# Two weight buffers of their own for the modulation vectors, fetched two ahead, and five instead of six for the rest

## Chip, cores and metric

The kernel runs on 1 core of one Trainium2 chip. The metric is the device time of one execution in microseconds (us), taken as the median of several runs.

## What is computed

The reference runs two blocks over a residual stream x of 256 tokens by 1024 features, with a second stream (the context) beside it, all in float32. Its parts are gated feed-forward networks (FFN), a short convolution mixer, a sparse attention that shares its keys and values ("kv"), a differential attention and a grouped-query attention. Each sublayer is modulated by vectors that come from a conditioning vector c:

```python
def modulate_pre(x, g_pre, shift, scale):
    return rms_norm(x, g_pre) * (1.0 + scale[:, None, :]) + shift[:, None, :]

def gated_post_add(x, y, g_post, gate, weight):
    return x + weight * gate[:, None, :] * rms_norm(y, g_post)

def swiglu_ffn(h, w_in, w_out):
    g, u = jnp.split(h @ w_in, 2, axis=-1)
    return (jax.nn.silu(g) * u) @ w_out

    shift, scale = jnp.split(jax.nn.silu(c) @ kv_ada_w + kv_ada_b, 2, axis=-1)
```

Shift, scale and gate are all products silu(c) @ W + b with W of 1024 by 1024 for each vector. The change concerns how these W (inputs `ada_w` and `kv_ada_w`) are brought in.

## The kernel before

**The large products** run on PE. A float32 weight block of 128 x 1024 (512 KB) is brought in by one DMA into a raw buffer (`raw_half`, line 237, issued from SP), split into a rounded high part by ACT (`whi`, line 246) and a remainder by DVE (`wlo`, line 247), and each product takes three matmuls: high by high, high by low and low by high (lines 492 to 494, 510 to 514). `slab` makes two such blocks and then calls `tick`. The raw pool has 6 buffers.

**The modulation vectors** are made on DVE. `gemv` puts eight steps for each vector in a queue, one for each block of 128 x 1024 of W; there are 32 vectors, 256 steps. A step is one scalar_tensor_tensor of DVE (line 176) for each condition: weight times `srow` (silu(c) on all partitions), summed along the row into one column of `vec`. 48 of the steps have two conditions, so line 176 issues 304 such instructions. The full product goes into a scratch tile `vjunk` (bf16, one buffer) that nobody reads. Sixteen more such instructions stand in `first_ffn` (line 311). After the eighth step a bias is added (line 180). `tick` adds credit at a rate that depends on the stage (`CFG`), and takes a step when there is enough; `need` forces the steps that are still missing when a vector is used. `step` uses the weight that the step before it had fetched, and fetches the next one (line 169 to 171), so one weight is on its way ahead. These fetches use the same raw pool and the same SP queue as the weights of the products.

**The order on each engine** is fixed when the program is built, by a scheduler that goes by priorities and free buffers; `slab` puts its loads and splits 36 places earlier (`early`). An engine carries out its instructions in that order, each waiting for its own inputs and buffers. SP issues nearly all weight DMAs, and its waits for a free raw buffer are in this queue as well. The context stream is woven into the main one by the program's writing (tiles with "ctx" in their name).

**Names in rows:** a00, a01, a02 are the first layer's FFN, convolution and FFN, kv the shared keys and values, a10, a11, a12 the second layer, diff0 the differential attention, bffn0 and bffn2 the FFNs of the second block, gqa its last attention. A tile's name has its stage and a running number. Lines touched: `step`, `fetch`, `tick` (152 to 182), pools (89 to 97), `first_ffn` (310), `grow` (369), `kv_cmp` (746), `late_setup` (1175).

## Time and profile before

| | |
|---|---|
| Median of 3 runs | 2145.55 us (2139.5 to 2145.56) |
| Profiled execution | 2140.95 us, of which the profiled span is 2139.2 us |
| Mean granted TensorE clock | 0.979 |
| PE busy | 2013.3 us, 94% of the span |
| DVE busy | 1625.5 us, 76% |
| ACT busy | 1087.3 us, 51% |
| DMA queue of the weights | 477.90 MB, 63.7% of 16 DMA engines |

The profile gives, for each engine, busy time and the idle time before an instruction with the work that ended it. A share of the span is an average over stages; the rows further below are from single places.

### The profile page before, as it was taken

The numbers are of one execution on the slowest core, as the hardware profiler recorded it, in microseconds if no ns is written. First come the engines' busy times: TensorE is split into PE (matmuls) and PEld (weight loads), VectorE is DVE, ScalarE is ACT, GpSimd is POOL, SyncE is SP. The second block draws the span as 40 slices with busy tenths as digits, with TensorE's granted clock in tenths as the row PEclk, the third lists the DMA queues.
The fourth block names the chain that finished last, engine by engine and source line by source line (L and its number), as shares of the span: only waits on it lengthen the run. The fifth ranks groups of instructions, "written<-read, shape, count | busy, mean of one in ns | idle before, by whom it ended". The sixth has DMA issues, their size and how long they took to land. (4 is left out here: it accounts for less than half of the span.)

```text
span 2139.2 us, 34672 instructions
## 1 busy us (share of the span) xinstructions
PE 2013.3 (94%) x13158; PEld 1796.2 (84%) x13158; DVE 1625.5 (76%) x2753; ACT 1087.3 (51%) x1769; POOL 133.6 (6%) x188
## 2 busy tenths in 40 slices
PE   6999899999899899899999999999999998989998
PEld 5998797998789788787788989877789997768998
DVE  7878898777877688878978666789888656866554
ACT  4444545443444466656765444547754444555443
POOL 0000201000200000110000000210010001100000
PEclk9999999999999999989999999999999999999999
DMA  8989697988677766544566866554359755414553
GB/s 332 330 309 355 236 327 277 330 292 291 222 258 276 241 230 210 195 157 138 190 238 232 292 221 237 180 207 148 128 207 342 264 191 178 140 53 150 188 186 118
DMA packets 136327, 486.46 MB, mean 227 GB/s; under 512 B 14976, under 2 KB 16480, under 8 KB 135392
## 3 DMA queue, kind: packets, MB, share of 16 engines
q1 hardware_dynamic: 134240, 477.90, 63.7%
q0 software_dynamic: 1728, 6.29, 0.8%
q8 instruction: 103, 1.69, 0.3%
q14 instruction: 64, 0.52, 0.1%
q10 hardware_dynamic: 192, 0.05, 0.0%
HBM read 480.47 MB, written 3.19 MB: 226 GB/s over the span
## 5 line engine op out<-in xcount | busy, mean ns | idle before, releaser
L1049 ACT ACT_TABLE_LOAD x15 | 19.2, 1283 | 6.6 <-DVE dst.diff0.2984_16079 L1047 1.7
L340 ACT ACT_TABLE_LOAD x13 | 16.7, 1283 | 0.2
L273 PE MATMUL ps.a00.6_101<-ident,x 128*128 128x128 f32 x4 | 1.1, 427 | 13.8 <-DMA x<-in_x 13.8
L375 POOL DMA_DIRECT2D G.bffn0.3378_18457<-row.bffn0.3377_18455 x1 | 0.6, 595 | 198.4 <-DMA row.bffn0.3377_18455<-diag.bffn0.3376_18453 198.4
L273 PEld LDWEIGHTS ps.a00.6_101<-ident,x 128*128 128x128 f32 x4 | 0.7, 216 | 13.7 <-issue 13.7
L375 POOL DMA_DIRECT2D G.a02.1032_5643<-row.a02.1031_5641 x1 | 0.6, 595 | 182.2 <-DMA row.a02.1031_5641<-diag.a02.1030_5639 182.2
L734 ACT ACTIVATE chunk.kv.1231_6595<-chunk.kv.1128_6071,cols 128x60 f32<-128x60 f32 x32 | 9.8, 387 | 4.0 <-PE ps.a10.1253_6672 L744 4.0
L375 POOL DMA_DIRECT2D G.a12.2528_13717<-row.a12.2527_13715 x1 | 0.6, 595 | 180.2 <-DMA row.a12.2527_13715<-diag.a12.2526_13713 180.2
L333 ACT ACT_TABLE_LOAD x9 | 11.5, 1283 | 0.2
L375 POOL DMA_DIRECT2D G.bffn2.3890_21467<-row.bffn2.3889_21465 x1 | 0.6, 595 | 171.6 <-DMA row.bffn2.3889_21465<-diag.bffn2.3888_21463 171.6
L401 POOL TENSOR_TENSOR rv.ctx.354_2048<-ss.ctx.352_2044,epsd 128x1 f32<-128x1 f32 x1 | 0.2, 191 | 169.8 <-ACT junk.ctx.351_2043 L394 169.8
L375 POOL DMA_DIRECT2D G.a11.2165_11615<-row.a11.2164_11613 x1 | 0.5, 530 | 116.9 <-DMA row.a11.2164_11613<-diag.a11.2163_11611 116.9
L484 ACT CAST chunk.a01.490_2583<-chunk.a01.492_2585 128x256 fp32r<-128x256 f32 x8 | 3.2, 406 | 8.9 <-DVE chunk.a01.492_2585 L676 8.9
L287 PE MATMUL ps.a00.38_198<-chunk.a00.20_148,chunk.a00.34_188 128*128 128x256 f32 x8 | 3.2, 401 | 4.8 <-ACT chunk.a00.34_188 L299 2.9
L386 POOL TENSOR_TENSOR rr.ctx.1396_7610<-rv.ctx.1395_7608,nhalf 128x8 f32<-128x8 f32 x1 | 1.6, 1637 | 87.7 <-DVE rv.ctx.1395_7608 L382 87.7
L176 DVE SCALAR_TENSOR_TENSOR vjunk.a12.2456_13210<-raw.a12.2435_13097,srow 128x1024 bf16<-128x1024 f32 x1 | 1.2, 1226 | 7.4 <-DMA raw.a12.2435_13097<-in_ada_w 7.4
L287 PEld LDWEIGHTS ps.a00.38_198<-chunk.a00.20_148,chunk.a00.34_188 128*128 128x128 f32 x8 | 2.0, 254 | 5.7 <-ACT chunk.a00.34_188 L299 3.2
L982 PE MATMUL ps.ctx.1412_7672<-ident,chunk.ctx.453_2431 128*128 128x128 f32 x4 | 1.1, 428 | 5.9 <-DVE chunk.ctx.453_2431 L962 5.9
L869 ACT ACT_TABLE_LOAD x5 | 6.4, 1283 | 0.1
L492 PE MATMUL ps.a10.1241_6626<-chunk.kv.1219_6556,whi.a10.1244_6630 128*128 128x256 f32 x8 | 3.1, 392 | 3.1 <-ACT whi.a10.1244_6630 L246 3.1
L982 PEld LDWEIGHTS ps.ctx.1412_7672<-ident,chunk.ctx.453_2431 128*128 128x128 f32 x4 | 0.7, 218 | 6.3 <-issue 6.3
L386 POOL TENSOR_TENSOR rqc<-rv.ctx.1316_7145,nhalf 128x8 f32<-128x8 f32 x1 | 1.6, 1637 | 62.0 <-DVE rv.ctx.1316_7145 L382 62.0
(11975 smaller groups left out, 9434.4 us busy)
## 6 DMA issues: line engine op xcount, KB each, us to landing
srow<-in_crow SPq DMA_DIRECT2D x3, 512.0 KB, 4.6
x<-in_x SPq DMA_DIRECT2D x1, 1024.0 KB
xc<-in_ctx SPq DMA_DIRECT2D x1, 1024.0 KB
kvd<-chunk.ctx.452_2429 SPq DMA_DIRECT2D x1, 1024.0 KB, 8.3
kvd<-chunk.ctx.451_2428 SPq DMA_DIRECT2D x1, 1024.0 KB
chunk.diff0.2745_14861<-kvd SPq DMA_DIRECT2D x1, 1024.0 KB
chunk.diff0.2746_14862<-kvd SPq DMA_DIRECT2D x1, 1024.0 KB
out<-x SPq DMA_DIRECT2D x2, 512.0 KB, 2.6
```

Of the source, the lines that this page charges most:

```text
L273: nc.tensor.transpose(ps[:, k, t * P:(t + 1) * P], self.x[:, t, kt * P:(kt + 1) * P], self.ident)
L287: mm(out, whi[:, ks], hi[:, k], start=(k == 0), stop=False)
L333: nc.scalar.activation(sg, gate, AF.Silu)
L340: nc.scalar.activation(sg, gate, AF.Silu)
L375: nc.gpsimd.dma_start(G, src.to_broadcast([P, D]))
L386: nc.gpsimd.tensor_tensor(r, v, self.nhalf[:, 0:n], op=ALU.pow)
L484: nc.scalar.copy(hi, src)
L492: mm(out, shi, mhi, start=first, stop=False)
L734: nc.scalar.activation(bt[:, j], self.kv2[i][:, :, 2 * j:2 * j + 16 * (NCMP - 1) + 1:16], AF.Identity, bias=self.col("pos", 16 * i + j, 1))
L869: nc.scalar.activation(p[:, br], p[:, br], AF.Exp, bias=mx[:, par, br:br + 1], accum_out=sm[:, br, par:par + 1])
L982: nc.tensor.transpose(ps[:, j, :], src[:, j * P:(j + 1) * P], self.ident)
L1049: nc.scalar.activation(e[:, :nk], ps[:, :nk], AF.Exp, bias=st[:, m:m + 1], scale=r, accum_out=st[:, 2 + m:3 + m])
```

## The change

The weights of the modulation vectors get a pool `vraw` with two buffers. `fetch` now fills a list of up to two weights and is called at the start and at the end of `step`, so two weights are on their way; the DMAs stay on SP (line 167 of the changed kernel). The load of weight n+2 waits until the last scalar_tensor_tensor on weight n is done. The raw pool of the other weights goes from 6 to 5 buffers. The scratch product is written over the weight itself, in float32, or, for the first of two conditions, into a tile `G` (two buffers, shared with the gate rows of `grow`). To make room, `vjunk` is gone, `diag` goes from two buffers to one, and the tile `misc` is replaced by a slot of `sg`, the tile that the FFN's gating uses. Numbers of instructions stay the same on every engine.

```diff
--- before.py
+++ after.py
@@ -87,7 +87,8 @@
         self.tc, self.nc, self.I, self.out, self.dbg = tc, tc.nc, I, out, dbg or {}
         pool = lambda name, bufs, **k: ctx.enter_context(tc.tile_pool(name=name, bufs=bufs, **k))
         self.cp = pool("consts", 1)
-        self.rawp = pool("raw", 6)
+        self.rawp = pool("raw", 5)
+        self.vrawp = pool("vraw", 2)
         self.splitp = pool("split", 4)
         self.arena = pool("arena", 12)
         self.wk = pool("work", 2)
@@ -97,7 +98,7 @@
         self.ph = "setup"
         self.vec = {}
         self.queue = []
-        self.fetched = None
+        self.fetched = []
         self.started = False
         self.credit = 0.0
         self.filler = None
@@ -153,28 +154,30 @@
         if self.started:
             self.credit += self.cfg["rates"].get(self.ph, self.cfg["rate"]) * n
         for _ in range(2):
-            nxt = self.fetched[3] if self.fetched else self.queue[0][3] if self.queue else None
+            nxt = self.fetched[0][3] if self.fetched else self.queue[0][3] if self.queue else None
             if self.hold or nxt is None or self.credit < len(nxt):
                 return
             self.credit -= len(nxt)
             self.step()
 
     def fetch(self):
-        if not self.queue:
-            return None
-        src, j, key, conds, vs = self.queue.pop(0)
-        return self.raw_half(src[j]), j, key, conds, vs
+        while self.queue and len(self.fetched) < 2:
+            src, j, key, conds, vs = self.queue.pop(0)
+            raw = self.vrawp.tile([P, 1024], F32, tag="vraw", name=self.name("vraw"))
+            self.nc.sync.dma_start(raw, src[j])
+            self.fetched.append((raw, j, key, conds, vs))
 
     def step(self):
         nc = self.nc
-        raw, j, key, conds, vs = self.fetched or self.fetch()
-        self.fetched = self.fetch()
+        self.fetch()
+        raw, j, key, conds, vs = self.fetched.pop(0)
         if not vs:
             vs.extend(self.cp.tile([P, KT], F32, name=self.name("vec")) for _ in conds)
-        for (cond, bias), v in zip(conds, vs):
-            junk = self.w([P, D], "vjunk", bufs=1, dt=BF16)
+        for n, ((cond, bias), v) in enumerate(zip(conds, vs)):
+            junk = raw if n == len(conds) - 1 else self.w([P, D], "G", bufs=2)
             nc.vector.scalar_tensor_tensor(junk, raw, 1.0, self.srow(cond), op0=ALU.mult, op1=ALU.mult,
                                            accum_out=v[:, j:j + 1])
+        self.fetch()
         if j == KT - 1:
             for i, ((cond, bias), v) in enumerate(zip(conds, vs)):
                 nc.vector.tensor_tensor(v, v, bias, op=ALU.add)
@@ -307,8 +310,7 @@
             a, b = ab[:, k, 1:2], ab[:, k, 0:1]
             for v in range(2):
                 raw = raws[2 * k + v] if 2 * k < len(raws) else self.raw_half(I["ada_w"][v][k])
-                junk = self.w([P, D], "vjunk", bufs=1, dt=BF16)
-                nc.vector.scalar_tensor_tensor(junk, raw, 1.0, srow, op0=ALU.mult, op1=ALU.mult,
+                nc.vector.scalar_tensor_tensor(raw, raw, 1.0, srow, op0=ALU.mult, op1=ALU.mult,
                                                accum_out=ab[:, k, v:v + 1])
             bb, ba = (self.col("ada_b", v * 8 + k, 1) for v in range(2))
             nc.vector.tensor_tensor(b, b, bb, op=ALU.add)
@@ -366,7 +368,7 @@
             v = gc
         ps = self.ps([KT, P], tag)
         nc.tensor.transpose(ps, v, self.ident)
-        vt = self.w([P, P], "diag", bufs=2)[:KT]
+        vt = self.w([P, P], "diag", bufs=1)[:KT]
         nc.scalar.copy(vt, ps)
         row = self.dram.tile([KT, P], F32, name=self.name("row"))
         nc.scalar.dma_start(row, vt)
@@ -743,7 +745,7 @@
                     o = (j % 4) * 256 + m * P
                     nc.tensor.matmul(ps[:, m, :], raws[j // 4][:, o:o + P], bt[:, j].rearrange("p g n -> p (g n)"),
                                      start=(j == 0), stop=(j == 15))
-            tt = self.w([P, 256], "misc", bufs=1)
+            tt = self.w([P, 2 * T], "sg", bufs=2)[:, 0:256]
             t1 = tt[:, 0:2 * n4].rearrange("p (m n) -> p m n", m=2)
             t2 = tt[:, 128:128 + 2 * n4].rearrange("p (m n) -> p m n", m=2)
             nc.scalar.activation(t1, ps, AF.Square)
@@ -1172,7 +1174,7 @@
         nc.sync.dma_start(self.xc, I["ctx"])
         self.rows = self.cp.tile([P, 384], F32, name="rows")
         nc.sync.dma_start(self.rows, I["rows"][:, 0:384].to_broadcast([P, 384]))
-        self.lrows = self.w([P, 256], "misc", bufs=1)
+        self.lrows = self.w([P, 2 * T], "sg", bufs=2)[:, 0:256]
         nc.sync.dma_start(self.lrows, I["rows"][:, 384:640].to_broadcast([P, 256]))
         self.lam()
```

In SP's queue in the FFN a02, before (`raw` of `in_ada_w` are modulation weights):

```order
295 L237 DMA raw.a02.1005_5467<-in_ada_w 128x1024
296 L237 DMA raw.a02.1007_5519<-in_ffn_w_in 128x1024
297 L237 DMA raw.a02.1010_5525<-in_ffn_w_in 128x1024
298 L237 DMA raw.a02.1013_5531<-in_ada_w 128x1024
299 L237 DMA raw.a02.1015_5535<-in_ada_w 128x1024
300 L237 DMA raw.a02.1018_5593<-in_ffn_w_out 128x1024
301 L237 DMA raw.a02.1021_5599<-in_ffn_w_out 128x1024
302 L237 DMA raw.a02.1024_5605<-in_ada_w 128x1024
```

and after:

```order
290 L240 DMA raw.a02.860_5229<-in_ffn_w_in 128x1024
291 L167 DMA vraw.a02.872_5307<-in_ada_w 128x1024
292 L240 DMA raw.a02.866_5294<-in_ffn_w_out 128x1024
293 L167 DMA vraw.a02.881_5348<-in_ada_w 128x1024
294 L240 DMA raw.a02.869_5300<-in_ffn_w_out 128x1024
295 L167 DMA vraw.a02.888_5411<-in_ada_w 128x1024
296 L240 DMA raw.a02.875_5335<-in_ffn_w_in 128x1024
297 L167 DMA vraw.a02.889_5414<-in_ada_w 128x1024
298 L240 DMA raw.a02.878_5341<-in_ffn_w_in 128x1024
299 L167 DMA vraw.a02.898_5484<-in_ada_w 128x1024
```

Of these, raw.a02.1005, 1013 and 1015 (first to third modulation load here) answer to vraw.a02.872, 881 and 888. The modulation loads now stand further ahead of the weights beside which they are used, and a load of each kind follows the other.

DVE in the differential attention, before (rows 1803 to 1807 are one row sum's way to the scaling of the scores):

```order
1802 L247 TENSOR_TENSOR wlo.diff0.2999_16148<-raw.diff0.2997_16145,whi.diff0.2998_16147 128x1024
1803 L1047 TENSOR_TENSOR dst.diff0.2962_15975<-dst.diff0.2962_15975,rqx 128x1
1804 L1079 TENSOR_SCALAR dst.diff0.2962_15975<-dst.diff0.2962_15975 128x1
1805 L1057 RECIPROCAL dst.diff0.2962_15975<-dst.diff0.2962_15975 128x1
1806 L1058 SCALAR_TENSOR_TENSOR dst.diff0.2962_15975<-dst.diff0.2962_15975,lam.ctx.350_2038 128x1
1807 L1060 SCALAR_TENSOR_TENSOR chunk.diff0.2749_14867<-chunk.diff0.2749_14867,dst.diff0.2962_15975 128x512
1808 L341 TENSOR_TENSOR sg.ctx.2964_16015<-sg.ctx.2964_16015,fps.ctx.2955_15930 128x256
1809 L384 SCALAR_TENSOR_TENSOR rv.diff0.2967_16029<-dst.diff0.2927_15787 128x1
```

and the same place after (rows 1817 to 1824 answer to 1803 to 1807):

```order
1816 L250 TENSOR_TENSOR wlo.diff0.2758_15911<-raw.diff0.2756_15908,whi.diff0.2757_15910 128x1024
1817 L1049 TENSOR_TENSOR dst.diff0.2723_15740<-dst.diff0.2723_15740,rqx 128x1
1818 L183 TENSOR_TENSOR vec.bffn0.2876_16496<-vec.bffn0.2876_16496,cols 128x8
1819 L178 SCALAR_TENSOR_TENSOR vraw.bffn0.2905_16686,vec.bffn0.2913_16752<-vraw.bffn0.2905_16686,srow_6768 128x1024
1820 L1081 TENSOR_SCALAR dst.diff0.2723_15740<-dst.diff0.2723_15740 128x1
1821 L1059 RECIPROCAL dst.diff0.2723_15740<-dst.diff0.2723_15740 128x1
1822 L178 SCALAR_TENSOR_TENSOR vraw.bffn0.2906_16689,vec.bffn0.2913_16752<-vraw.bffn0.2906_16689,srow_6768 128x1024
1823 L1060 SCALAR_TENSOR_TENSOR dst.diff0.2723_15740<-dst.diff0.2723_15740,lam.ctx.301_1993 128x1
1824 L1062 SCALAR_TENSOR_TENSOR chunk.diff0.2517_14639<-chunk.diff0.2517_14639,dst.diff0.2723_15740 128x512
1825 L343 TENSOR_TENSOR sg.ctx.2725_15780<-sg.ctx.2725_15780,fps.ctx.2716_15695 128x256
1826 L386 SCALAR_TENSOR_TENSOR rv.diff0.2728_15794<-dst.diff0.2689_15553 128x1
```

Two modulation steps for the FFN that follows (bffn0) and a bias now stand within that chain. Counted by the weight split that they follow, 17 line-176 steps lay before between 1380 and 1550 us and 34 do after; 6 and 13 between 1550 and 1600; 23 and 1 between 1600 and 1675; 4 and 8 between 962 and 1003.

SP in the shared kv, before (lines 710 and 711 shift a result and wait for the product; `in_kv_b` are weights of the next product):

```order
338 L710 DMA chunk.kv.1128_6071<-chunk.kv.1127_6068 64x255
339 L711 DMA chunk.kv.1128_6071<-chunk.kv.1127_6068 64x256
340 L237 DMA raw.kv.1166_6306<-in_kv_b 128x1024
341 L710 DMA chunk.kv.1128_6071<-chunk.kv.1127_6068 64x255
342 L711 DMA chunk.kv.1128_6071<-chunk.kv.1127_6068 64x256
343 L237 DMA raw.kv.1169_6312<-in_kv_b 128x1024
344 L237 DMA raw.kv.1172_6318<-in_ada_w 128x1024
345 L237 DMA raw.kv.1174_6322<-in_ada_w 128x1024
```

and after:

```order
334 L240 DMA raw.kv.1009_6028<-in_kv_b 128x1024
335 L240 DMA raw.kv.1016_6100<-in_kv_b 128x1024
336 L240 DMA raw.kv.1019_6106<-in_kv_b 128x1024
337 L240 DMA raw.kv.1026_6170<-in_kv_b 128x1024
338 L167 DMA vraw.kv.1056_6316<-in_ada_w 128x1024
339 L167 DMA vraw.kv.1057_6319<-in_ada_w 128x1024
340 L240 DMA raw.kv.1029_6176<-in_kv_b 128x1024
341 L695 DMA chunk.kv.993_5938<-in_cmp_w 128x256
342 L240 DMA raw.kv.1042_6262<-in_kv_v 128x1024
343 L712 DMA chunk.kv.994_5941<-chunk.kv.993_5938 64x255
```

The loads of `in_kv_b` all stand ahead of the shifts now (lines 712 and 713 after).

## Rows read from the trace of the kernel before

**Rows 1.** the page: spans, busy time and share of each engine.

```profile
PE 2013.3 (94%) x13158; PEld 1796.2 (84%) x13158; DVE 1625.5 (76%) x2753; ACT 1087.3 (51%) x1769; POOL 133.6 (6%) x188
```

**Rows 2.** waits of PE, ended by the releaser named: us, times, longest.

```profile
PE ps.ctx.1412_7672 L982 <- DVE chunk.ctx.453_2431 L962: 5.9, 1, 5.9
PE ps.diff0.2743_14849 L982 <- DVE chunk.diff0.2616_14186 L975: 4.4, 1, 4.4
...
PE ps.a10.1241_6626 L492 <- ACT whi.a10.1244_6630 L246: 3.1, 1, 3.1
...
PE ps.a02.722_3847 L511 <- DVE wlo.a02.1061_5797 L247: 2.5, 1, 2.5
...
PE ps.a12.2421_13023 L494 <- DVE wlo.a12.2425_13028 L247: 1.7, 1, 1.7
...
PE ps.kv.1176_6326 L492 <- ACT whi.kv.1167_6308 L246: 1.2, 1, 1.2
...
PE ps.a02.722_3847 L511 <- DVE wlo.a02.994_5422 L247: 1.0, 1, 1.0
...
PE fps.ctx.454_2432 L511 <- DVE wlo.ctx.468_2493 L247: 0.2, 1, 0.2
```

**Rows 3.** waits of DVE, the largest and the smallest of 49 on modulation weights.

```profile
DVE vjunk.a12.2456_13210 L176 <- DMA raw.a12.2435_13097<-in_ada_w: 7.4, 1, 7.4
...
DVE vjunk.a02.1073_5846 L176 <- DMA raw.a02.1070_5840<-in_ada_w: 5.3, 1, 5.3
...
DVE vjunk.ctx.1943_10379 L176 <- DMA raw.ctx.1904_10164<-in_ada_w: 1.1, 1, 1.1
```

**Rows 4.** timeline of SP, end of the FFN a02 (start, duration).

```profile
538.44 0.33 SPq L237 DMA_DIRECT2D raw.a02.1070_5840<-in_ada_w  x1
```

**Rows 5.** timeline of DVE, end of the FFN a02 (idle before, in brackets).

```profile
546.03 1.23 DVE L176 SCALAR_TENSOR_TENSOR vjunk.a02.1073_5846<-raw.a02.1070_5840,srow 128x1024 bf16<-128x1024 f32 x1 [5.34 <-DMA raw.a02.1070_5840<-in_ada_w]
...
547.18 1.22 DVE L247 TENSOR_TENSOR wlo.a02.1061_5797<-raw.a02.1059_5794,whi.a02.1060_5796 128x1024 fp32r<-128x1024 f32 x1
```

**Rows 6.** timeline of DVE, context attention and FFN a10 (as above).

```profile
738.24 1.23 DVE L176 SCALAR_TENSOR_TENSOR vjunk.a10.1453_7875<-raw.a10.1438_7784,srow 128x1024 bf16<-128x1024 f32 x1 [4.44 <-DMA raw.a10.1438_7784<-in_ada_w]
...
743.70 0.69 DVE L957 TENSOR_TENSOR chunk.ctx.453_2431<-fps.ctx.1357_7389,rr.ctx.1396_7610 128x512 f32<-128x512 f32 x1 [1.23 <-POOL rr.ctx.1396_7610 L386]
```

**Rows 7.** 5 us stretches: PE, PEld, DVE, ACT, POOL busy; clock; DMA share.

```profile
545.00:550.00 5.00, 2.53 (x9) 1.73 (x8) 3.94 (x7) 1.00 (x2) 0.00 (x0) 0.83 0.58 220
740.00:745.00 5.00, 0.47 (x3) 0.05 (x1) 3.77 (x8) 1.29 (x2) 2.03 (x2) 0.78 0.29 105
745.00:750.00 5.00, 3.10 (x10) 2.05 (x11) 4.08 (x7) 0.59 (x1) 2.09 (x1) 0.50 0.30 110
750.00:755.00 5.00, 5.00 (x32) 5.00 (x31) 4.22 (x11) 3.41 (x7) 0.00 (x0) 0.69 0.86 297
1245.00:1250.00 5.00, 3.24 (x25) 2.90 (x24) 4.67 (x7) 0.29 (x1) 0.00 (x0) 1.00 0.44 142
```

**Rows 8.** timeline of SP, shared kv (start, duration).

```profile
590.53 0.54 SPq L237 DMA_DIRECT2D raw.kv.1166_6306<-in_kv_b  x1
```

**Rows 9.** stretches, all work (columns as in rows 7).

```profile
962.00:1003.00 41.00, 35.93 (x219) 26.39 (x217) 38.27 (x99) 27.89 (x79) 2.99 (x7) 0.99 0.39 131
...
1380.00:1550.00 170.00, 156.61 (x989) 132.01 (x989) 143.64 (x318) 107.47 (x201) 17.81 (x19) 0.98 0.47 163
1550.00:1600.00 50.00, 47.18 (x265) 39.29 (x262) 39.28 (x67) 29.09 (x55) 6.54 (x10) 1.00 0.58 200
1600.00:1675.00 75.00, 74.47 (x532) 70.38 (x533) 66.73 (x93) 31.69 (x34) 0.00 (x0) 1.00 0.94 333
```

**Rows 10.** same stretches, line 176 alone, two instructions a slice (DVE only).

```profile
1380.00:1550.00 170.00, 20.88 (x34) 0.98 0.47 163
...
1600.00:1675.00 75.00, 29.68 (x49) 1.00 0.94 333
```

**Rows 11.** waits of SP's queue on the first compression layer.

```profile
SPq L237 <- PE ps.a10.1253_6672 L744: 8.4, 4, 6.3
```

## Prediction

> **What bounds the kernel.** I read the page first: PE is busy for 94% of the span, DVE for 76% [rows 1]. Without PE's idle time of 2139.2 - 2013.3 = 126 us the kernel could not be faster except through the clock, so each term below is a piece of this idle time or of PE's time at the lower clock. Next come the waits of DVE [rows 3]: 49 waits of 1.1 us or more for a modulation weight make 105.9 us, the largest 7.4 us. This is what the change aims at, but it is DVE's idle time. What counts is how much of it comes out at PE. The waits of PE [rows 2] name a split (`whi` or `wlo`) as the last releaser 24 times, from 3.1 down to 0.2 us, together 21.9 us, and two longer ones, 5.9 and 4.4 us, which end with a step of DVE (head normalisation and rotation in the attentions). So at most about a quarter of the 105.9 us reaches PE. The rest is hidden, because DVE runs some microseconds ahead of PE.
>
> One place shows the mechanism end to end. SP issued a modulation weight at 538.44 us [rows 4], its step on DVE began at 546.03 after 5.34 us idle, and the split behind it began only at 547.18 [rows 5]. A matmul that needed that split waited 2.5 us [rows 2]. DVE works in order, so a late vector weight stops a weight split that had its data.
>
> **The change part by part.**
>
> *Two buffers and two ahead.* In the FFN a02 the loads now stand further ahead of their steps, with a product weight or none between. Five PE waits there name a `wlo` behind such a step: the first 2.5, the last 1.0 us, together 6.8. From the issue at 538.44 to the use at 546.03 were 7.6 us [rows 4, 5], of which DVE waited 5.3. Between two steps stand two or three instructions of up to 1.2 us, so a load that is one step further ahead has some 4 us more with the step itself, which covers all but about one microsecond of the largest wait and the whole of the others. I take 6.0 of the 6.8. After the largest wait the granted clock was 0.83 over 5 us [rows 7]: 0.85 us if PE had worked throughout, and it was busy for half, so 0.5 more. Gain **6.5** (0 to 7.7).
>
> *The attention of the context, 746 us.* DVE waited 4.44 us for a modulation weight at 738.24 us; the head normalisation queued behind it, with one stop of 1.23 us on POOL at 743.70 [rows 6]; PE then waited 5.9 us [rows 2]. Without the first wait PE's is 5.9 - 4.4 = 1.5 us. The clock fell as well: 0.50 from 745 to 750 with 3.10 us of PE work and 0.69 from 750 to 755 [rows 7]. Of 3.7 us after the wait half was lost (1.8) and of 5 us 31% (1.6), 3.4 in all. Around the 1.7 us wait at 1246 us it stayed at 1.00 [rows 7], so a wait of 1.5 us should leave it up. Gain **7.8** (0 to 9.3).
>
> *1246 us.* The 7.4 us wait [rows 3] left PE only 1.7 us idle [rows 2]. Gain **1.5** (0 to 1.7).
>
> *Shared kv.* The split weight of `in_kv_b` was issued at 590.53 us behind shifts that wait for the product [rows 8]; three PE waits follow, the largest 1.2 us, together 2.3. Those loads now stand ahead of the shifts. Gain **2.0** (0 to 2.3).
>
> *The other splits.* 21.9 less 6.8, 1.7, 2.3 and the 3.1 of the compression layer (next) leave 8.0 us in small pieces. Some follow vector weights and some product weights. Gain **3.0** (0 to 8.0).
>
> *Five buffers instead of six.* A modulation weight took one or two of the six, so the products keep as many as they had except where there are no modulation loads. At the end (bffn0 onwards) PE is at 74.47 of 75 us in the last stretch of [rows 9] and only the last tens of loads lose a place; I cost this at nothing, covered by that lead. Exception: the compression layer holds four raw buffers until its matmuls are done, and SP waited there 8.4 us in four waits [rows 11]; PE waited 3.1 us for `whi.a10.1244` [rows 2]. One free buffer instead of two makes the next weights pass singly. Loss **2** (0, as the modulation loads no longer take a place, to 6.3, one more wait like the longest of the four).
>
> *The steps that move.* The scheduler puts the steps where a buffer and an idle DVE allow it. They now come earlier: 17 more between 1380 and 1550 us, 7 more from 1550 to 1600, 22 fewer from 1600 to 1675, 4 more from 962 to 1003. Each is 1.23 us [rows 5]; before, 17 of them took 20.88 us in that stretch [rows 10]. Taking them out of 1600 to 1675 gains nothing: PE is busy for 74.47 of 75 us there. In the differential attention DVE had 170 - 143.64 = 26.4 us idle [rows 9], and gets 17 x 1.23 = 20.9 us more: 97% busy. Its chain there is row sum, reciprocal, scaling, transposing on PE, and a step now stands inside it. If DVE's idle time takes all of it the cost is 0; if none, 20.9. The nearest row is 962 to 1003 us: at 38.27/41 = 93% DVE, PE is idle for 5.1 us, or 12% [rows 9]. Now it is 13.4 of 170, or 8%; at 12% it would be 21. Loss **7**. From 1550 to 1600 8.6 us go into 10.7 idle: nothing. From 962 to 1003, 4 x 1.23 = 4.9 into 2.7 idle: loss **2**. Against this stands the wait of 4.4 us of PE at 1434 us [rows 2], which follows vector weights too; I leave it as the lower end of this term, so -4.4 to 20.9.
>
> *Scratch in place, float32.* A step that writes bf16 takes 1.23 us, a subtract of two float32 tiles that writes a 4-byte result 1.22 [rows 5], so the wider result costs nothing. The Trainium skill, Vector Engine (DVE) Microarchitecture Reference, "Points that are easy to get wrong", says that a scalar_tensor_tensor with two non-bf16 SBUF sources has half the throughput; the 1.23 against 1.22 us do not show it. By that page the steps that move would cost twice as much, an estimate of 42 us for 17 of them, and rows decide against it.
>
> *The wait that is added* is SP's: the load n+2 waits for step n, and product weights queue behind it. It waited before for a raw buffer in the same way. The scratch in `G` (48 steps), one `diag` and the shared `sg` can wait for a slot; `diag` is used once for a gate, tens of microseconds apart, so the cover is PE's queue. Cost 0; above, one wait like a02's 2.5 us [rows 2], below nothing, since no wait is taken away.
>
> **Sum.** 6.5 + 7.8 + 1.5 + 2 + 3 = 20.8 gained, 7 + 2 + 2 = 11 lost: about 10 us less. From the profiled execution, 2140.95: 2131. The median of the runs is 4.6 above it, so the runs should show **2135**.
>
> **Rivals.**
> - *A larger gain.* DVE's idle time takes in the moved steps, 1434 us is gained too, and most of the 8 us of small pieces: 20.8 + 4.4 + 3 - 2 = 26, so 2119. For it: DVE's waits for weights are part of the 26.4 us idle. Against: 97% busy in a chain. The Trainium skill, Perfetto Trace Analysis, "Optimization Strategy", reads consistent bubbles as a possible lack of buffers; by that alone all 21.9 us of split waits and more would go. The waits in a02 agree, the 93% row of DVE does not.
> - *No change.* PE is 94% busy, and the next late thing (POOL's reciprocal root, 1.23 us at 743.70; attention chains) takes the freed time: half of 20.8 less 11 is a loss of 0.6, so 2146.
> - *Slower, by DVE in the differential attention.* All 24 steps moved to 1380 to 1600 us cost their full 1.23 us, because each delays a scaling that PE waits for: 29.5, with 2 and 2 for the others, against 20.8: 13 slower, 2158. It decides once the loss there passes 17 us (20.8 - 4 = 16.8).
> - *It doesn't do what it says.* SP reaches the load n+2 late, since step n itself is late, and the vector wait remains at half its size: the gain shrinks to 10, the losses stay, 2146.
>
> **Chances.** My forecast 0.36; larger gain 0.17; no change 0.20; held up on SP 0.05; slower 0.22. About 0.3% (6.4 us) is what a measurement here can tell, so faster is below 2139 and the first two cases make 0.53; no change and SP 0.25; slower 0.22. The range goes from 2115 (gains in full, little lost) to 2156; most of its upper end belongs to the slower rival. The likeliest case alone is 2127 to 2140.
>
> **What would show it.** Right: waits of DVE for modulation weights fall from 105.9 to under 50 us; the PE wait at 746 us falls to some 1.5 us with the clock at 1.00 behind it; the five waits in a02 and the kv waits go; DVE is over 90% busy in the differential attention and PE idle there grows by up to 10 us. Wrong: the same waits remain under the new names (SP held), or PE's waits for DVE in the differential attention grow by more than 17 us, or the freed waits come back on POOL and ACT behind the same matmuls.

## The result and the profile after

The changed kernel takes **2172.39 us** (median of 4 runs, 2169.11 to 2174.21) against 2145.56 of the kernel before (2139.5 to 2148.36): ratio 1.0127, 95% interval 1.0102 to 1.0152. It is 27 us slower. The forecast was 2135, in a range of 2115 to 2156.

The profiled execution has a span of 2172.1 us (before 2139.2) and a mean granted clock of 0.965 (0.979). It is the slowest of its four runs, and the profiled one of before is among the faster, so traces show 33 us of difference where the medians show 27. Busy time on the page (ACT carries out two instructions more than before; the other counts are the same):

```profile
PE 2031.4 (94%) x13158; PEld 1813.6 (83%) x13158; DVE 1624.1 (75%) x2753; ACT 1090.7 (50%) x1771; POOL 143.2 (7%) x188
```

Against [rows 1], PE's idle time is 2172.1 - 2031.4 = 140.7 us, 15 more, and its busy time 18 us longer for the same 13158 matmuls at a lower mean clock; so of the 33 us between the two spans more than half is matmuls that took longer. The waits of PE (us in total, times, longest):

```profile
PE ps.a00.401_2413 L449 <- DVE x L642: 5.8, 1, 5.8
PE ps.a11.2027_11687 L449 <- DVE x L642: 5.4, 1, 5.4
PE ps.a01.611_3655 L449 <- DVE x L642: 3.7, 2, 3.5
PE ps.a02.962_5822 L449 <- DVE x L642: 3.5, 1, 3.5
PE ps.diff0.2511_14621 L984 <- DVE chunk.diff0.2386_13960 L977: 3.3, 1, 3.3
...
PE ps.a02.821_4980 L496 <- DVE wlo.a02.832_5048 L250: 2.1, 1, 2.1
...
PE ps.ctx.1252_7516 L984 <- DVE chunk.ctx.392_2374 L964: 1.5, 1, 1.5
```

What is new stands at the top. Four waits for `x`, the residual add of DVE at the end of a stage of the first block (line 642, before 640), make 18.4 us; before, all waits for `x` made 3.6 us and none was over 1.2. What the change aimed at did shrink: the 24 waits for splits, 21.9 us in all [rows 2], are now 17 with 13.1 us, and the 5.9 us wait at the context's attention is 1.5 us, what the prediction had for it. DVE's waits of 1.1 us or more for modulation weights [rows 3] went only from 49 with 105.9 us to 46 with 93.3 us.

One of the four places, from the attention a11 to the FFN a12. DVE (start, duration, idle before):

```profile
1143.27 0.69 DVE L638 TENSOR_TENSOR ps.a11.1968_11424<-ps.a11.1968_11424,G.a11.1966_11420 128x512 f32<-128x512 f32 x1
1143.87 1.22 DVE L250 TENSOR_TENSOR wlo.ctx.2021_11648<-raw.ctx.2019_11645,whi.ctx.2020_11647 128x1024 fp32r<-128x1024 f32 x1
1149.57 1.23 DVE L178 SCALAR_TENSOR_TENSOR vraw.a12.2083_11956<-vraw.a12.2083_11956,srow 128x1024 f32<-128x1024 f32 x1 [4.49 <-DMA vraw.a12.2083_11956<-in_ada_w]
...
1151.86 0.69 DVE L638 TENSOR_TENSOR ps.a11.1979_11469<-ps.a11.1979_11469,G.a11.1966_11420 128x512 f32<-128x512 f32 x1
1152.46 0.74 DVE L642 SCALAR_TENSOR_TENSOR x<-ps.a11.1968_11424,rr.a11.2005_11597,x 128x512 f32<-128x512 f32 x1
```

and SP, which issues the loads of the modulation weights:

```profile
1132.25 0.33 SPq L167 DMA_DIRECT2D vraw.a12.2072_11883<-in_ada_w  x1
...
1137.07 0.33 SPq L167 DMA_DIRECT2D vraw.a12.2073_11886<-in_ada_w  x1
...
1141.23 0.42 SPq L167 DMA_DIRECT2D vraw.a12.2083_11956<-in_ada_w  x1
```

The step on `vraw.a12.2083` waits 4.49 us for its weight, and the product with the gate (line 638) and the residual add (line 642) stand behind it. Its load takes the buffer of `vraw.a12.2072`, two loads earlier, so it could go out only when that step was done (1138.45 us and 1.2 us long); SP issued it at 1141.23, and it was used 8.3 us later. PE had nothing but this add to go on with, waited 5.4 us, and then worked at half clock. Before, no step stood at this place; DVE waited for ACT and for the row sum:

```profile
1129.97 0.70 DVE L636 TENSOR_TENSOR ps.a11.2180_11666<-ps.a11.2180_11666,G.a11.2165_11615 128x512 f32<-128x512 f32 x1 [0.51 <-ACT junk.a11.2209_11793 L635]
1130.94 0.75 DVE L640 SCALAR_TENSOR_TENSOR x<-ps.a11.2167_11619,rr.a11.2210_11798,x 128x512 f32<-128x512 f32 x1 [0.28 <-POOL rr.a11.2210_11798 L403]
```

The other three places are not like this one. While PE waited there, DVE stood idle for a modulation weight for 1.06 us at the end of a00, and not at all at the ends of a01 and a02 (waits of 0.75 to 1.78 us for a weight stand some microseconds ahead of them). Otherwise it worked, on steps whose weight had come and on weight splits that the scheduler had put between the two halves of the add. At the end of a00:

```profile
224.99 1.21 DVE L250 TENSOR_TENSOR wlo.ctx.397_2380<-raw.ctx.395_2377,whi.ctx.396_2379 128x1024 fp32r<-128x1024 f32 x1
226.12 1.22 DVE L178 SCALAR_TENSOR_TENSOR vraw.a00.347_2151<-vraw.a00.347_2151,srow 128x1024 f32<-128x1024 f32 x1
...
228.40 1.23 DVE L178 SCALAR_TENSOR_TENSOR vraw.a00.355_2219<-vraw.a00.355_2219,srow 128x1024 f32<-128x1024 f32 x1 [1.06 <-DMA vraw.a00.355_2219<-in_ada_w]
```

Three steps, none of them late, stood ahead of this add in the kernel before too. So the late load is shown as the main part of the wait at a11 alone; at the other boundaries the order of the work on DVE has a part that the traces do not separate.

The clock, in 5 us stretches of the change (columns as in [rows 7]):

```profile
650.00:655.00 5.00, 5.00 (x25) 5.00 (x25) 4.47 (x9) 4.30 (x14) 0.00 (x0) 0.50 0.32 110
...
665.00:670.00 5.00, 5.00 (x25) 5.00 (x25) 1.74 (x5) 2.08 (x5) 1.34 (x1) 0.50 0.72 233
765.00:770.00 5.00, 4.08 (x17) 3.18 (x16) 5.00 (x9) 1.76 (x3) 0.00 (x0) 0.56 0.51 190
1150.00:1155.00 5.00, 1.75 (x8) 1.57 (x8) 5.00 (x9) 1.58 (x5) 0.28 (x2) 0.63 0.46 146
1155.00:1160.00 5.00, 4.43 (x12) 3.37 (x11) 5.00 (x9) 1.96 (x6) 2.56 (x6) 0.50 0.32 130
```

After the boundary at 1150 us it is 0.63 and 0.50. In the stretches behind the other three waits it is 0.50, 0.50 and 0.69. In the compression layer it stayed at 0.50 or 0.62 from 645 to 670 us, with PE at 5.00 of 5 us in four of the five stretches (the first and the last of those are shown); before, it was at 0.52 and 0.80 there, for 10 us. From the kv's 9th weight split to the 17th of a10, before and after:

```profile
603.10:704.60 101.50, 95.97 (x640) 88.03 (x638) 73.96 (x116) 50.16 (x89) 4.29 (x2) 0.97 0.74 269
613.20:726.50 113.30, 109.02 (x685) 100.96 (x685) 79.55 (x129) 51.31 (x91) 3.23 (x2) 0.89 0.71 243
```

PE is idle for less time than before there (4.3 against 5.5 us), and the stretch is 11.8 us longer at a mean clock of 0.89 instead of 0.97. By the 5 us stretches the lower clock takes 11.8 us of PE's work here and 3.3 before, an estimate; 45 matmuls more, which the order puts into this stretch, make the rest. So most of the loss in this stage is the clock, and it is not longer waiting.

To see where the time goes I took the start of the nth weight split of a stage on DVE from the timelines of both traces; the difference is how late the change is at that point. Two experiments stand beside it. All four columns are of one profiled execution each; that of the run with the steps kept out is the fastest of its four (2160.68 us), that of the change its slowest.

| split | before, us | change | steps out of boundaries | one pool of seven |
|---|---|---|---|---|
| a00, 57th | 220 | -3.1 | -1.3 | +0.9 |
| a01, 1st | 238 | +6.1 | +3.4 | -0.6 |
| a01, 29th | 326 | +7.8 | +4.1 | -0.2 |
| a02, 1st | 345 | +16.4 | +5.8 | -0.2 |
| a02, 65th | 550 | +9.8 | -0.8 | -4.8 |
| kv, 1st | 567 | +15.2 | -0.8 | -1.4 |
| kv, 9th | 603 | +10.1 | -1.8 | -5.7 |
| a10, 17th | 705 | +21.8 | +15.5 | -8.7 |
| a10, 65th | 887 | +13.0 | +7.5 | -13.7 |
| a11, 17th | 1123 | +19.3 | +8.7 | -6.9 |
| a12, 1st | 1143 | +23.9 | +8.7 | -6.7 |
| a12, 65th | 1326 | +22.3 | +6.1 | -9.1 |
| bffn0, 1st | 1582 | +33.1 | +11.2 | -5.6 |
| bffn0, 29th | 1682 | +33.2 | +20.5 | -7.3 |
| bffn2, 65th | 2120 | +32.9 | +19.7 | -3.9 |

The change loses at the four boundaries (9.2, 8.6, 5.4 and 4.6 us, 27.8 in all), in the compression layer (11.7, kv 9th to a10 17th), in a11 and in the differential attention (10.8, a12 65th to bffn0 1st), and gains in the FFNs a02 (6.6) and a10 (8.8). From bffn0 on the two kernels run alike. A single row is good to some microseconds, since the order on DVE differs.

A second measure comes from the same timelines: the median time from the issue of a modulation weight (272 loads) to the start of its step. It was 7.08 us before and is **6.15 us** after. The product weights' (603 loads, to the start of the high part on ACT) stayed, 11.67 and 11.75 us. SP's own waits before it could issue a modulation load, summed over the trace, went from 343 to 479 us (408 in the pool of seven below, which is fast all the same).

### The profile page after: what moved, and what is told of

Same layout as the page of the kernel before. It is cut to its first block, busy times and chain, and to the rows that moved or that the text cites. A ratio compares the mean times of both kernels' runs of the same rounds, so it can differ in the third digit from the quotient of the medians.

```text
span 2172.1 us, 34556 instructions
## 1 busy us (share of the span) xinstructions
PE 2031.4 (94%) x13158; PEld 1813.6 (83%) x13158; DVE 1624.1 (75%) x2753; ACT 1090.7 (50%) x1771; POOL 143.2 (7%) x188
## 5 line engine op out<-in xcount | busy, mean ns | idle before, releaser
L276 PE MATMUL ps.a00.6_104<-ident,x 128*128 128x128 f32 x4 | 1.1, 428 | 13.7 <-DMA x<-in_x 13.7
L736 ACT ACTIVATE chunk.kv.1084_6452<-chunk.kv.994_5941,cols 128x60 f32<-128x60 f32 x32 | 10.6, 389 | 4.2 <-issue 4.0
L276 PEld LDWEIGHTS ps.a00.6_104<-ident,x 128*128 128x128 f32 x4 | 0.7, 217 | 13.7 <-issue 13.7
```

The costliest lines, as they stand in the source:

```text
L276: nc.tensor.transpose(ps[:, k, t * P:(t + 1) * P], self.x[:, t, kt * P:(kt + 1) * P], self.ident)
L736: nc.scalar.activation(bt[:, j], self.kv2[i][:, :, 2 * j:2 * j + 16 * (NCMP - 1) + 1:16], AF.Identity, bias=self.col("pos", 16 * i + j, 1))
```

## Experiments

Theory A: modulation steps with late loads stand in front of the residual adds. Theory B: the products miss their sixth buffer. Theory C: DVE is too full in the differential attention. Theory A' is A with the cause that the table's second measure points to: a load can go out only when its own buffer is free. Times are medians of the runs with their lowest and highest; the kernel before was run beside each group (2141.5 to 2145.5 us).

**Five buffers alone.** On the kernel before:

```diff
-        self.rawp = pool("raw", 6)
+        self.rawp = pool("raw", 5)
```

> The kernel before with five raw buffers instead of six and nothing else. Theory A (modulation steps whose loads land late stand ahead of the residual adds at the stage boundaries, PE idles there and its clock falls behind it): nothing of that is here, so 2141 to 2152 us, and PE's waits for the residual adds of x stay under 4 us in all. Theory B (the products miss the sixth buffer): most of the 27 us of the change, 2162 to 2175 us, with PE's waits for weight splits above the 21.9 us of before.

Measured: 2174.6 us (2173.42 to 2176.82), ratio 1.0139 (1.0121 to 1.0158). As slow as the change, as theory B had it, but at other places: PE's waits for `x` are 8.5 us, those for splits 29.9 us in 36. Of its waits of PE:

```profile
PE ps.kv.1164_6254 L494 <- DVE wlo.kv.1156_6237 L247: 3.2, 1, 3.2
...
PE ps.a10.1765_9477 L447 <- DVE x L640: 3.1, 1, 3.1
```

The median from issue to use fell for both kinds, to 6.03 us (modulation) and 8.63 us (products). So this is a kernel with too few buffers for everything, and it doesn't yet tell what the change lacks.

**Steps held at the boundaries.** On the change, at the end of `before_last` in `run` (the hold is lifted at the end of `boundary`):

```diff
+                self.hold = True
```

> The change, but no modulation step is taken by credit between the point where a stage of the first block has its next gate and the end of its boundary; the steps come later, none is left out. Theory A: the four waits of PE for residual adds (18.4 us in the change) fall under 8 us and the low-clock stretches behind them go, 2145 to 2160 us. Theory B or theory C (DVE is too full in the differential attention): the boundaries of the first block decide nothing, 2168 to 2176 us.

Measured: 2174.8 us (2172.51 to 2176.09). This was no test. The scheduler took the first steps of the next stage instead and put them at the same place, and their loads were late too. DVE at the boundary from a01 to a02:

```profile
353.51 1.23 DVE L178 SCALAR_TENSOR_TENSOR vraw.a02.644_3768<-vraw.a02.644_3768,srow 128x1024 f32<-128x1024 f32 x1 [4.53 <-DMA vraw.a02.644_3768<-in_ada_w]
...
354.66 0.69 DVE L638 TENSOR_TENSOR ps.a01.562_3446<-ps.a01.562_3446,G.a01.552_3404 128x512 f32<-128x512 f32 x1
355.27 0.74 DVE L642 SCALAR_TENSOR_TENSOR x<-ps.a01.554_3408,rr.a01.584_3562,x 128x512 f32<-128x512 f32 x1
```

The waits of PE for `x` stayed at 17.4 us. At the end of a00 no step stood within 13 us of the add's end this time, and PE waited 4.8 us there in two waits all the same.

**Steps really kept out.** As the run before, and each step multiplies by a one made from the residual after its last add:

```diff
             diags.append(self.norm_r(x, t))
+        self.one = self.w([P, 1], "one", bufs=2)
+        self.nc.vector.tensor_scalar(self.one, x[:, TT - 1, D - 1:D], 0.0, 1.0, op0=ALU.mult, op1=ALU.add)
...
-            nc.vector.scalar_tensor_tensor(junk, raw, 1.0, self.srow(cond), op0=ALU.mult, op1=ALU.mult,
+            nc.vector.scalar_tensor_tensor(junk, raw, self.one, self.srow(cond), op0=ALU.mult, op1=ALU.mult,
```

> The change with the steps really kept out of the boundaries of the first block: held by credit as in the earlier run, and each later step multiplies by a one that a small DVE instruction makes from the residual after its last add, so that no step can be placed ahead of the adds. If late steps in front of the adds cost time (theory A'): the waits of PE for x fall from 18.4 to under 5 us and the time to 2145 to 2162 us, where the rest is the products' missing buffer. If the late loads only show there and come back elsewhere: 2165 to 2178 us.

Measured: 2164.94 us (2160.68 to 2165.51), 7 us faster than the change, on the border of the two forecasts. Waits of PE:

```profile
PE ps.a10.1094_6482 L498 <- ACT whi.a10.1097_6486 L251: 10.7, 1, 10.7
PE ps.a00.395_2398 L453 <- DVE x L646: 4.8, 2, 3.1
...
PE ps.a11.2025_11680 L453 <- DVE x L646: 0.6, 1, 0.6
```

At a11 the wait for `x` is 0.6 instead of 5.4 us; all waits for `x` are 10.8 us (21.4 in the change), and the four at the boundaries 6.3 us, where the forecast was under 5. At the end of a00 4.8 of 5.8 us stay without any step. The table shows both halves: the kernel is 15 us ahead of the change at a12, 22 us at bffn0, and gives 9 back in bffn0, into which the steps were pushed. It waits 10.7 us for a split in the compression layer. By the table the four boundaries now lose 6.4 instead of 27.8 us. So steps in front of the adds, late or not, cost some 15 us up to a12 in these two executions, but keeping them out moves part of the work elsewhere: the medians are only 7 us apart.

**One pool of seven.** On the change, `vraw` goes, and `fetch` uses `raw_half`:

```diff
-        self.rawp = pool("raw", 5)
-        self.vrawp = pool("vraw", 2)
+        self.rawp = pool("raw", 7)
```

> The change, with its 5 + 2 buffers as one raw pool of seven that both kinds of weights share; two ahead, and the scratch in place, stay. If the limit of two own buffers makes the steps late (theory A): the waits for residual adds fall under 6 us, 2130 to 2148 us. If fetching two ahead itself, or the scratch in place, is the cost: 2162 us or more. Theory B also says fast here, since the products can have more than five.

Measured: **2136.47 us** (2127.6 to 2142.26), ratio to before 0.9968 (0.9946 to 0.999). The same seven buffers as the change, the same two loads ahead, 36 us less. It has the faster time that both theories forecast for it, so it shows that the division costs the time, not which of its two sides. Issue to use is 8.56 us, DVE's waits of 1.1 us or more for modulation weights 60.6 us in 31. Waits of PE for `x` are 7.7 us (forecast under 6):

```profile
PE ps.a02.962_5819 L447 <- DVE x L640: 3.7, 1, 3.7
...
PE ps.a11.2027_11684 L447 <- DVE x L640: 1.0, 1, 1.0
```

With the steps kept out of the boundaries as well:

> One pool of seven, two ahead, and the steps kept out of the boundaries as in the first of these runs. If steps in front of the residual adds cost time with a shared pool too (PE waits 7.7 us for x there): 2115 to 2131 us. If their loads are early enough: 2132 to 2145 us.

2135.33 us (2132.8 to 2140.64), ratio 0.9974 (0.9961 to 0.9986): no further gain. With a shared pool the boundary is not the place to mend.

**One load ahead, or two.** In `fetch`:

```diff
-        while self.queue and len(self.fetched) < 2:
+        while self.queue and len(self.fetched) < 1:
```

In the change:

> The change with one load ahead instead of two, still in its two own buffers. Theory A: a load is issued later by a step, so steps at the boundaries wait as long or longer: 2168 to 2185 us, DVE's waits for modulation weights above the 83 us of the change. If it is the second load ahead that pushes product weights back in SP's queue, 2140 to 2160 us.

2162.85 us (2153.76 to 2167.56): faster by 9.5, against theory A's forecast. DVE's waits are as in the change (112.6 against 115.2 us, all counted; the 83 us of the forecast left out the short ones). In the pool of seven:

> One pool of seven for all weights, one load ahead as in the kernel before. With the 5 + 2 split one ahead was 9 us faster than two; if a second load ahead is no gain in a shared pool either: 2122 to 2138 us. If the second load ahead is what makes the pool of seven fast: 2141 us or more.

2144.73 us (2139.46 to 2154.8): slower by 8 than with two, against the forecast too. In a pool of six, two ahead:

> The change with one raw pool of six for both kinds of weights: the buffers of before, but two ahead and the scratch in place. Theory A': as the kernel before or a little faster, 2136 to 2150 us, the gain of the pool of seven (7 us) being the seventh buffer's or the second load's. If two ahead in a shared pool takes buffers from the products: 2155 us or more.

2150.15 us (2144.52 to 2153.55); and one ahead in six, which is the kernel before with the edits of memory alone:

> The kernel before with the edits of memory alone: scratch in place or in G, one diag, the shared sg; one pool of six, one load ahead. If these edits cost nothing, as the prediction had it: 2138 to 2149 us. If they are the 9 us that stayed between the two kernels without loads at six buffers: 2150 to 2160 us.

2143.98 us (2137.82 to 2157.28), ratio 1.0006 (0.9987 to 1.0026). So scratch in place, `G`, one `diag` and the shared `sg` cost nothing that these runs can tell. A second load ahead gave -8 us in seven shared, +6 in six shared, +9.5 in five and two. It does not change the lead: issue to use is 6.30 us with one ahead and 6.15 with two in 5 + 2, 8.42 and 8.56 in seven shared. In the profiled executions more than half of the difference lies in the compression layer, in the stretch of the two rows above, and goes with the clock: with one ahead and with two it takes 107.8 and 113.3 us at a mean clock of 0.97 and 0.89 in 5 + 2, 100.3 and 105.7 us at 0.98 and 0.90 in six, 107.4 and 98.5 us at 0.90 and 1.00 in seven. With one profile of each, this says where the time went; why the clock stays low there in some of them is not shown.

**Six and one.** On the change, one load ahead:

```diff
-        self.rawp = pool("raw", 5)
-        self.vrawp = pool("vraw", 2)
+        self.rawp = pool("raw", 6)
+        self.vrawp = pool("vraw", 1)
```

> Seven buffers again, but split 6 + 1: six raw buffers for the products, one for the modulation weights, one load ahead. Theory A' (a modulation load can go out only when its own buffer is free, so its lead is shorter than in a shared pool, and DVE waits for it in front of the residual adds): slower than 5 + 2 with one ahead (2163 us), 2175 to 2230 us, and the median time from issue to use of a modulation weight falls under 6 us. Theory B (the products lack the sixth buffer): 2140 to 2155 us.

2271.8 us (2267.81 to 2286.83). The direction is that of theory A', and the size more than its range. Issue to use is 4.52 us, and DVE waits for modulation weights before 176 steps. Where a vector is needed and its steps are missing, they run one by one, some 4.7 us apart from 232 to 279 us, and PE waits for the end:

```profile
PE fps.ctx.382_2342 L449 <- DVE htmp.ctx.322_2051 L461: 58.8, 1, 58.8
PE ps.a10.1588_9303 L449 <- DVE x L642: 37.9, 2, 33.5
```

**No modulation loads.** The step's loads are left out (134 MB by the pages, 486.4 against 352.2), and the step multiplies the resident row, so nothing here waits for a modulation weight after the first FFN's sixteen:

```diff
-            self.nc.sync.dma_start(raw, src[j])
...
-            nc.vector.scalar_tensor_tensor(junk, raw, 1.0, self.srow(cond), op0=ALU.mult, op1=ALU.mult,
+            nc.vector.scalar_tensor_tensor(junk, self.srow(0), 1.0, self.srow(cond), op0=ALU.mult, op1=ALU.mult,
```

> The change with the loads of the modulation weights by step left out (136 MB of 486 MB); each step multiplies the resident silu(c) row instead, so the modulation vectors are other numbers. Five raw buffers for the products stay. Theory A': no step waits, the waits for residual adds of x fall under 5 us, and the time goes below 2125 us. Theory B: the products still have five buffers, 2150 us or more.

> The kernel before with the same loads left out and the same replacement; six raw buffers for the products alone. Theory A': within 6 us of the change without these loads, since the 27 us between the two kernels come from these loads. Theory B: 15 us or more faster than the change without them.

> The change without the loads of the modulation weights, with six raw buffers for the products instead of five (one scratch tile is left of the two own buffers). If the 16 us between the two kernels without these loads are the sixth buffer's: 2090 to 2101 us. If they are the scratch in place, one diag or the shared sg: 2107 us or more.

Measured: the change 2111.08 us (2107.58 to 2115.88), the kernel before 2094.87 (2093.21 to 2095.89), the change with six raw buffers 2104.21 (2101.74 to 2112.73). The change came below 2125 as theory A' had it, but the two kernels are 16 us apart, which is theory B's forecast (15 or more) and not that of theory A' (within 6). The loads cost the change 61 us and the kernel before 51, so 11 of the 27 us are theirs. Of the 16 that stay, the sixth buffer has 7; the other 9 lie outside both forecasts. The edits of memory are free with loads, so it may be the order alone; that wasn't tried. In the profiled executions what the sixth buffer gains lies in the compression layer: the stretch used above takes 109.1 us with five raw buffers and 102.3 with six, at a mean clock of 0.95 and 1.00.

The other forecast of theory A' missed as well: the waits for `x` are 10.6 us in the change without the loads, not under 5, and 11.6 us in the kernel before without them. Its two largest in the change:

```profile
PE ps.a00.401_2365 L448 <- DVE x L641: 4.7, 2, 3.1
PE ps.a10.1589_9142 L448 <- DVE x L641: 3.1, 1, 3.1
```

Counted as in the table (against the kernel before with its loads), the four boundaries lose 10.5, 2.1, 2.3 and 0.0 us. So 14.9 of the 27.8 us there stay in a kernel whose steps wait for no load, most of it at the end of a00, and lateness isn't their cause.

**A buffer to the one or the other.** Three instead of four buffers for the split weights free 8 KB a partition, in which a sixth raw or a third `vraw` buffer fits:

```diff
-        self.splitp = pool("split", 4)
+        self.splitp = pool("split", 3)
```

> Control for the next two: the change with three instead of four buffers for the split weights (whi and wlo), which frees 8 KB a partition. Either theory: as the change or slower, 2168 to 2195 us.

> The control with six raw buffers for the products and two for the modulation weights. Theory B (products lack a buffer): 15 to 28 us faster than the control. Theory A' (the modulation weights' two buffers): 0 to 10 us faster, the waits of PE for x stay above 12 us, only those in the compression layer shrink.

> The control with five raw buffers for the products and three for the modulation weights (two loads ahead as before). Theory A': 12 to 28 us faster than the control, median time from issue to use of a modulation weight over 7.5 us, PE waits for x under 10 us. Theory B: 0 to 8 us faster.

Measured: 2195.38 us (2192.98 to 2197.61) for the control, 2188.91 (2183.68 to 2192.72) with 6 + 2, 2181.43 (2171.27 to 2183.75) with 5 + 3. The buffer is worth 14 us to the modulation weights and 6.5 to the products. Both times are in the ranges of theory A'; the products' share is more than nothing. Issue to use is 6.31, 6.39 and 8.00 us in this order. Waits of PE for `x` with 6 + 2, the two largest:

```profile
PE ps.a00.401_2413 L449 <- DVE x L642: 7.2, 2, 6.6
PE ps.a10.1589_9305 L449 <- DVE x L642: 4.5, 2, 4.1
```

and with 5 + 3, the same two:

```profile
PE ps.a10.1589_9305 L449 <- DVE x L642: 4.5, 2, 4.1
...
PE ps.a00.401_2413 L449 <- DVE x L642: 0.8, 1, 0.8
```

The wait at the first boundary is 0.8 us with the third `vraw` buffer, against 6.9 in the control and 7.2 with 6 + 2. Two smaller forecasts missed: all waits for `x` are 12.1 us with 5 + 3 (forecast under 10; 17.7 in the control), and with 6 + 2 nothing shrank in the compression layer, whose stretch takes 116.0 us against 116.2 in the control.

**What follows.** Tiles, arrangement and time, with four split buffers:

| buffers | one ahead | two ahead |
|---|---|---|
| 5 shared | 2174.6 | |
| 6 shared | 2141.5 to 2145.6 | 2150.2 |
| 7 shared | 2144.7 | 2136.5 |
| 5 + 2 | 2162.9 | 2172.4 |
| 6 + 1 | 2271.8 | |

Seven buffers divided 5 + 2 are slower than six that are shared. Theory C (DVE too full) has no run of its own; by the first table the differential attention has at most 10.8 of the 33 us.

## Why the prediction was wrong

**The step that failed** is the price of the two own buffers. The prediction said that a load "is one step further ahead" and so "has some 4 us more", and of the added wait of SP that "It waited before for a raw buffer in the same way", at "Cost 0". Neither holds. The list in `fetch` is two long, but the third load waits for a buffer that the first step must free, where before any of six would do. The median lead did not grow by 4 us but fell from 7.08 to 6.15 us, and DVE's waits for modulation weights stayed at 93.3 us, where the prediction's own sign of being right was under 50. A third own buffer gives a lead of 8.0 (from 6.31), a shared pool of seven 8.56.

**The place that was left out** is the boundary of a stage. The mechanism was right, a step stops what stands behind it on DVE, and I applied it to weight splits alone. At a boundary the thing behind it is the residual add that PE waits for: 18.4 us in four waits, and low clock behind each. The run with the steps kept out shows 15 us of this by a12. How much of it is lateness is shown only in part: at a11 a load of 4.49 us idle time stands in the wait, while without any loads about half of the boundary loss stays, from the order in which steps and splits were put in front of the adds. I counted moved steps by stretch, not by what they stand in front of.

**Point by point.**
- *FFN a02, gain 6.5.* Not for the reason given: the table has a gain of 6.6 us between the stage's first and 65th split, but PE's waits for splits there are still 6.0 us (6.8 before), with 2.1 and 2.0 as the largest, at other matmuls.
- *746 us, gain 7.8.* The wait fell from 5.9 to 1.5 us as worked out. The clock didn't follow: 0.56 in the stretch behind it, where I had 1.00 by the likeness to 1246 us. So 4.4 of the 7.8.
- *Shared kv, gain 2.0.* Right: the waits for its splits went from 2.3 to 0.7 us.
- *1246 us and the small splits, 4.5.* All waits for splits fell by 8.8 us, where the terms had 6.0 (a02) + 2.0 + 4.5 = 12.5.
- *Five buffers, loss 2 (0 to 6.3).* Undersized, its upper bound a little too low, and of another kind than priced. The table has 11.7 us in the compression layer, and SP waits 13.3 us in four there instead of 8.4 [rows 11] (4.8 instead of 7.7 at the second product). But PE's idle time fell there, and most of the loss is the lower clock (8.5 us by the estimate above), which the term did not have. The sixth buffer's price is 6.5 us (6 + 2 against its control) to 7 (without loads); only without loads is it seen to lie in this layer.
- *Differential attention, loss 7.* Right in kind and nearly in size. In a stretch of the same length as the one in [rows 9] PE did 4.3 us less and DVE is at 93%:

```profile
1402.00:1572.00 170.00, 152.34 (x939) 127.86 (x940) 157.94 (x341) 104.41 (x193) 21.14 (x18) 0.98 0.63 211
```

  By the table the loss is up to 10.8 us. The rival "slower, by DVE in the differential attention" had the right sign for a wrong place: it put 29.5 us on the moved steps.
- *Memory edits, 0.* Right: 2143.98 against 2143.45 us, and the interval of the ratio holds 1.

**The rivals.** "It doesn't do what it says" was the nearest one: DVE's waits for modulation weights fell by an eighth only, since the load waits for the step. I gave it 0.05 and 2146, with the losses unchanged; the losses at the boundaries and by the clock were missing from it.

**What stays open:** how the 27 us divide to the microsecond (loads 11, sixth buffer 7, 9 unassigned by the runs without loads; by the split-buffer runs the third modulation buffer is worth twice the sixth raw one); what keeps the clock low in the compression layer in some runs, with which the price of a second load ahead goes; the 6 us in a11. Every change of buffers also changes the order that the scheduler makes, so no run here changes a buffer alone.

## What to carry to other kernels

A private pool is a limit as well as a reserve: ask how many buffers each kind could have at its busiest in the shared pool, not how many it has on average, and try the shared pool with the same memory first (here 2136 against 2172 us). The lead of a load went here with the buffers it could take, not with how far ahead the program asked for it (6.15 and 6.30 us in two own buffers, 8.56 and 8.42 in seven shared, with two ahead and with one); measure it as issue to use. On an engine that works in order, look first at what stands in front of a result that the next engine waits for with nothing else to do, as at the stage boundaries here, and at the granted clock behind such a wait. Where a stage is slower, compare its idle time and its clock before naming a wait: in the compression layer it was mostly the clock.

## What the hardware showed that was not expected

The clock after a short wait of PE did not go by the wait's length alone. After 1.5 us of waiting at 764 us it fell to 0.56, and after 1.7 us at 1246 us in the kernel before it stayed at 1.00 [rows 7]; in the first case PE was busy for 3.48 us of the 5 us stretch in which the wait began and 4.08 of the next, in the second for 3.24 and 5.00. In the compression layer it stayed at the lower of its two levels, 1.2 GHz, for 20 us although PE is shown busy for 5.00 of 5 us; what would raise it there wasn't tried.
